# A batched matmul in fp16 on one core: loads six batches ahead, and stores on the loads' queue

## The chip, the core and the metric

The kernel runs on one core of one Trainium2 chip. The core has five engines that run side by side, each with its own stream of instructions: TensorE (PE; its weight loads are shown apart as PEld), VectorE (DVE), ScalarE (ACT), GpSimd (POOL) and SyncE (SP). They meet through semaphores. Tensors lie in HBM; compute reads on-chip memory, and the matmul's results come out in a second, small on-chip memory (PSUM). Data between HBM and the chip are moved by 16 DMA engines, which all five engines can ask for transfers through queues. The metric is the device time of one execution in microseconds (us); lower is better.

## The reference

```
batch, dim_i, dim_j, dim_k = 32, 256, 512, 384
x: (32, 256, 512) float32      y: (32, 512, 384) float32
return np.einsum('bij,bjk->bik', x, y).astype(np.float32)
```

There are 32 independent products of a 256x512 and a 512x384 matrix. Per batch 512 KB of x and 768 KB of y are read and 384 KB of output are written.

## The kernel before

There is one loop over the 32 batches (L43). A batch is handled in five steps.

1. Load. x of the batch goes into `x_sb` (L47), y into `y_sb` (L54), each as one DMA issued by SyncE. A partition, one of 128 rows of on-chip memory, holds two rows of x (4 KB) and four rows of y (6 KB), in either case one unbroken piece of HBM. For the last batch y is loaded as four DMAs, one for each t (L52).
2. Cast. The four slices of y become fp16 in `y_r`, two on ScalarE (L59), two on VectorE (L61).
3. Transpose. TensorE transposes eight 128x128 blocks of x through an identity matrix into PSUM (`t_ps`, L67). VectorE and ScalarE cast the results into `xt_sb` (L73, L75).
4. Multiply. Eight fp16 matmuls add up over t into two PSUM tiles `o_ps` (L84), which ScalarE (L93) and VectorE (L95) copy into `o_sb`.
5. Store. GpSimd issues one DMA of `o_sb` to HBM (L102). For the last batch there are two, one for each half (L100).

Every pool of the loop has eight buffers, apart from the two in PSUM, which have four. The program is written batch by batch, and a scheduler interleaves neighbouring batches on the engines: on VectorE, for instance, the casts of transposed x for one batch stand ahead of the casts of y for it. Each engine then goes through its own list in order and waits where an instruction names a semaphore. SyncE's list holds nothing but loads, GpSimd's (after the identity) nothing but stores.

The DMAs of SyncE use eight semaphores in turn, DMAHW0 to DMAHW7. So a DMA is issued only when the one eight places earlier on that queue has landed, and at most eight are under way. In before that is four batches of loads. GpSimd's stores have their own eight semaphores, DMASW0 to DMASW7.

Of the kernel before, what the change touches and what calls it, by code (L numbers as in the profile page):

```python
# [1 line left out]

# [5 lines left out]


MM_DT = mybir.dt.float16
P = 128


@with_exitstack
def kernel(
    ctx: ExitStack,
    tc: tile.TileContext,
    x: bass.AP,
    y: bass.AP,  # L20
    out: bass.AP,
):
    nc = tc.nc

    B, I, J = x.shape
    _, _, K = y.shape

    NI = I // P
    NJ = J // P

    const_pool = ctx.enter_context(tc.tile_pool(name="const", bufs=1))
    x_pool = ctx.enter_context(tc.tile_pool(name="x_pool", bufs=8))
    y_pool = ctx.enter_context(tc.tile_pool(name="y_pool", bufs=8))
    yr_pool = ctx.enter_context(tc.tile_pool(name="yr_pool", bufs=8))
    xt_pool = ctx.enter_context(tc.tile_pool(name="xt_pool", bufs=8))
    o_pool = ctx.enter_context(tc.tile_pool(name="o_pool", bufs=8))
    tpsum_pool = ctx.enter_context(tc.tile_pool(name="tpsum", bufs=4, space=bass.MemoryType.PSUM))
    opsum_pool = ctx.enter_context(tc.tile_pool(name="opsum", bufs=4, space=bass.MemoryType.PSUM))

    identity = const_pool.tile([P, P], mybir.dt.float32)  # L40
    make_identity(nc, identity)

    for b in range(B):  # L43
        last = b == B - 1

        x_sb = x_pool.tile([P, NI, J], mybir.dt.float32)
        nc.sync.dma_start(out=x_sb, in_=x[b].rearrange("(p r) j -> p r j", p=P))  # L47
        y_sb = y_pool.tile([P, NJ, K], mybir.dt.float32)
        y_src = y[b].rearrange("(q t) k -> q t k", q=P)
        if last:  # L50
            for t in range(NJ):
                nc.sync.dma_start(out=y_sb[:, t], in_=y_src[:, t])  # L52
        else:
            nc.sync.dma_start(out=y_sb, in_=y_src)  # L54

        y_r = yr_pool.tile([P, NJ, K], MM_DT)
        for t in range(NJ):
            if t % 2 == 0:
                nc.scalar.copy(y_r[:, t], y_sb[:, t])  # L59
            else:  # L60
                nc.vector.tensor_copy(y_r[:, t], y_sb[:, t])  # L61

        xt_sb = xt_pool.tile([P, NJ, NI, P], MM_DT)
        for t in range(NJ):
            t_ps = tpsum_pool.tile([P, NI, P], mybir.dt.float32)
            for r in range(NI):
                nc.tensor.transpose(  # L67
                    t_ps[:, r],
                    x_sb[:, r, t::NJ],
                    identity,  # L70
                )
            if t % 2 == 0:
                nc.vector.tensor_copy(xt_sb[:, t], t_ps)  # L73
            else:
                nc.scalar.copy(xt_sb[:, t], t_ps)  # L75

        o_sb = o_pool.tile([P, NI, K], mybir.dt.float32)
        o_ps = [
            opsum_pool.tile([P, K], mybir.dt.float32, name=f"o_ps_{r}", tag="o_ps")
            for r in range(NI)  # L80
        ]
        for t in range(NJ):
            for r in range(NI):
                nc.tensor.matmul(  # L84
                    o_ps[r],
                    xt_sb[:, t, r],
                    y_r[:, t],
                    start=(t == 0),
                    stop=(t == NJ - 1),
                )  # L90
        for r in range(NI):
            if r % 2 == 0:
                nc.scalar.copy(o_sb[:, r, :], o_ps[r])  # L93
            else:
                nc.vector.tensor_copy(o_sb[:, r, :], o_ps[r])  # L95

        out_dst = out[b].rearrange("(p r) k -> p r k", p=P)
        if last:
            for r in range(NI):
                nc.gpsimd.dma_start(out=out_dst[:, r], in_=o_sb[:, r])  # L100
        else:
            nc.gpsimd.dma_start(out=out_dst, in_=o_sb)  # L102


# [1 line left out]
_INS = ['x', 'y']  # L106
_OUTS = [((32, 256, 384), 'float32')]


# [23 lines left out]
```

## Time and profile before

| what | us |
|---|---|
| the runs shown | 140.85, 142.6, 140.8 |
| their median | 140.85 |
| span of the profiled execution, first to last instruction | 139.8 |
| median of the runs less that span | 1.05 |
| PE busy | 90.5 |
| ACT busy | 67.9 |
| DVE busy | 60.5 |

The times listed don't say which run was profiled; the span stands for it. The profile is of one execution. Its page gives the busy time of each engine, a row of 40 slices of the span with the busy share of each in tenths, the DMA queues with their packets, megabytes and share of the 16 DMA engines' time, the chain of work that ended last, the costliest groups of instructions, and the DMA issues with the median time from issue to landing. Other views list the waits (who waited for whom: us in total, times, longest), the instructions in order of time (start, us, engine, line), and the busy time of each engine in chosen stretches. In this last one a row begins with the stretch and its length; then come PE, PEld, DVE, ACT and POOL busy with their counts, the clock that TensorE was granted, the DMA share and GB/s. `SPq` and `POOLq` are the queues of SyncE and GpSimd.

### The profile page before, as it was taken

The page shows a single profiled execution, that of the slowest core. Times are in us where ns is not written, and L with a number is a line of the kernel's source. Part 1 is how long each engine was busy: PE and PEld are TensorE (multiplying, and loading weights), DVE is VectorE, ACT ScalarE, POOL GpSimd, SP SyncE. Part 2 cuts the span into 40 slices and gives each one's busy share as a digit, 9 for nine tenths or more (in the row PEclk, how much of TensorE's full clock was granted, in tenths as well). Part 3 has the DMA queues.
Part 4 walks back from the last instruction along what each step waited for, and adds up shares of the span by engine and source line. Part 5 has one row for each costly group of instructions (what it writes and reads, how often), then busy time and mean ns, then how long its engine had stood idle before and what let it go on. Part 6 is the DMA issues. An engine that isn't in the chain of part 4 may idle for free.

```text
span 139.8 us, 1774 instructions
## 1 busy us (share of the span) xinstructions
PE 90.5 (65%) x512; PEld 64.6 (46%) x512; DVE 60.5 (43%) x160; ACT 67.9 (49%) x161; POOL 18.6 (13%) x39
## 2 busy tenths in 40 slices
PE   0699755477763776774777676776558777764820
PEld 0467543355541554552655444554446355553500
DVE  0346542455541555442555542455534255555420
ACT  3347633446632465453556544465634355565610
POOL 1002210111110111101111110111110111111130
PEclk9999999959999599998699997799997579999996
DMA  4999999999999999999999999999999999999631
GB/s 185 412 426 356 362 410 424 424 417 424 423 412 424 416 416 419 427 416 420 413 423 417 424 416 421 423 414 420 425 419 412 419 421 420 420 422 403 270 155 70
DMA packets 12266, 54.65 MB, mean 391 GB/s; under 512 B 1600, under 2 KB 2112, under 8 KB 12256
## 3 DMA queue, kind: packets, MB, share of 16 engines
q1 hardware_dynamic: 9648, 41.95, 73.9%
q0 software_dynamic: 2608, 12.59, 21.9%
q8 instruction: 4, 0.07, 0.2%
q14 instruction: 6, 0.05, 0.1%
HBM read 41.94 MB, written 12.58 MB: 390 GB/s over the span
## 4 chain that ended last, share of the span: by engine, by line
DMA 87%; issue 5%; PE 3%; SPq 1%; POOL 1%; ACT 0%; POOLq 0%
DMA y_sb<-in_y_dram 87%; PE o_ps L84 1%; PE t_ps L67 1%; SPq L47 1%; SPq L54 0%; POOL out_dram L100 0%; POOL out_dram L102 0%; POOLq L128 0%; ACT y_r L59 0%; ACT xt_sb L75 0%; POOLq L100 0%
## 5 line engine op out<-in xcount | busy, mean ns | idle before, releaser
L84 PE MATMUL o_ps<-y_r,xt_sb 128*128 128x384 f16 x256 | 52.2, 349 | 38.2 <-ACT y_r L59 37.1
L84 PEld LDWEIGHTS <-xt_sb 128*128 128x128 f16 x256 | 25.8, 102 | 57.4 <-issue 40.2
L67 PE MATMUL t_ps<-identity,x_sb 128*128 128x128 f32 x256 | 42.7, 318 | 5.4 <-DMA x_sb<-in_x_dram 5.2
L67 PEld LDWEIGHTS t_ps<-identity,x_sb 128*128 128x128 f32 x256 | 39.2, 213 | 11.7 <-PE o_ps L84 5.9
L95 DVE COPY o_sb<-o_ps 128x384 f32<-128x384 f32 x32 | 17.8, 557 | 48.8 <-issue 36.8
L59 ACT CAST y_r<-y_sb 128x384 f16<-128x384 f32 x64 | 29.8, 511 | 17.0 <-DMA y_sb<-in_y_dram 16.8
L102 POOL DMA_DIRECT2D out_dram<-o_sb x31 | 16.9, 545 | 114.1 <-DVE xt_sb L73 72.8
L93 ACT COPY o_sb<-o_ps 128x384 f32<-128x384 f32 x32 | 15.3, 478 | 33.6 <-issue 26.4
L75 ACT CAST xt_sb<-t_ps 128x256 f16<-128x256 f32 x64 | 23.6, 372 | 15.3 <-PE t_ps L67 12.9
L61 DVE CAST y_r<-y_sb 128x384 f16<-128x384 f32 x64 | 20.5, 361 | 22.3 <-DMA y_sb<-in_y_dram 21.8
L73 DVE CAST xt_sb<-t_ps 128x256 f16<-128x256 f32 x64 | 25.4, 417 | 3.2 <-PE t_ps L67 2.8
L59 ACT ACT_TABLE_LOAD x1 | 1.3, 1283 | 0.7 <-PEq L117 0.7
L100 POOL DMA_DIRECT2D out_dram<-o_sb x2 | 1.1, 539 | 2.5 <-ACT o_sb L93 2.5
masks.py:199 POOL TENSOR_SCALAR_AFFINE_SELECT identity<-identity 128x128 f32<-128x128 f32 x1 | 0.3, 287 | 0.1
masks.py:197 POOL MEMSET identity<- 128x128 f32 x1 | 0.2, 204 | 0.3 <-POOLq L117 0.3
L117 POOL MEMSET const-float32-0.0<- 128x1 f32 x1 | 0.1, 98 | 0.2 <-issue 0.2
L117 POOL MEMSET const-bfloat16-1.0<- 128x1 bf16 x1 | 0.1, 101 | 0.0
L117 POOL MEMSET const-uint8-127<- 128x1 uint8 x1 | 0.1, 101 | 0.0
L117 POOL MEMSET const-float32-1.0<- 128x1 f32 x1 | 0.1, 98 | 0.0
## 6 DMA issues: line engine op xcount, KB each, us to landing
y_sb<-in_y_dram SPq DMA_DIRECT2D x31, 768.0 KB, 16.1
x_sb<-in_x_dram SPq DMA_DIRECT2D x32, 512.0 KB, 16.1
out_dram<-o_sb POOLq DMA_DIRECT2D x31, 384.0 KB, 6.4
y_sb<-in_y_dram SPq DMA_DIRECT2D x4, 192.0 KB, 13.1
out_dram<-o_sb POOLq DMA_DIRECT2D x2, 192.0 KB, 2.2
```

The lines of the kernel that those rows point to most:

```text
L47: nc.sync.dma_start(out=x_sb, in_=x[b].rearrange("(p r) j -> p r j", p=P))
L59: nc.scalar.copy(y_r[:, t], y_sb[:, t])
L61: nc.vector.tensor_copy(y_r[:, t], y_sb[:, t])
L67: nc.tensor.transpose(t_ps[:, r], x_sb[:, r, t::NJ], identity,)
L73: nc.vector.tensor_copy(xt_sb[:, t], t_ps)
L75: nc.scalar.copy(xt_sb[:, t], t_ps)
L84: nc.tensor.matmul(o_ps[r], xt_sb[:, t, r], y_r[:, t], start=(t == 0), stop=(t == NJ - 1),)
L93: nc.scalar.copy(o_sb[:, r, :], o_ps[r])
L95: nc.vector.tensor_copy(o_sb[:, r, :], o_ps[r])
L100: nc.gpsimd.dma_start(out=out_dst[:, r], in_=o_sb[:, r])
L102: nc.gpsimd.dma_start(out=out_dst, in_=o_sb)
L117: nc = _bacc.Bacc("TRN2", target_bir_lowering=False, num_devices=1)
```

## The change

Loads, compute and store of a batch become three functions. Before the loop, loads 0 and 1, the identity matrix, and loads 2 to 5 are issued. Then, for each batch b, the loads of batch b+6 are issued, batch b is computed, and its store is issued, now by SyncE. x and y have nine buffers instead of eight, `y_r` and `xt_sb` four instead of eight. The last batch is no longer cut: its y is one load, its output one store. The arithmetic is untouched.

```diff
-    x_pool = ctx.enter_context(tc.tile_pool(name="x_pool", bufs=8))
-    y_pool = ctx.enter_context(tc.tile_pool(name="y_pool", bufs=8))
-    yr_pool = ctx.enter_context(tc.tile_pool(name="yr_pool", bufs=8))
-    xt_pool = ctx.enter_context(tc.tile_pool(name="xt_pool", bufs=8))
+    x_pool = ctx.enter_context(tc.tile_pool(name="x_pool", bufs=AHEAD + 3))
+    y_pool = ctx.enter_context(tc.tile_pool(name="y_pool", bufs=AHEAD + 3))
+    yr_pool = ctx.enter_context(tc.tile_pool(name="yr_pool", bufs=4))
+    xt_pool = ctx.enter_context(tc.tile_pool(name="xt_pool", bufs=4))
...
-    make_identity(nc, identity)
-    for b in range(B):
-        last = b == B - 1
...
-        nc.sync.dma_start(out=x_sb, in_=x[b].rearrange("(p r) j -> p r j", p=P))
...
-        if last:
-            for t in range(NJ):
-                nc.sync.dma_start(out=y_sb[:, t], in_=y_src[:, t])
-        else:
-            nc.sync.dma_start(out=y_sb, in_=y_src)
+    def load(b):
+        x_sb = x_pool.tile([P, NI, J], F32, name="x_sb")
+        y_sb = y_pool.tile([P, NJ, K], F32, name="y_sb")
+        x_src = x[b].rearrange("(p r) j -> p r j", p=P)
+        y_src = y[b].rearrange("(q t) k -> q t k", q=P)
+        nc.sync.dma_start(out=x_sb, in_=x_src)
+        nc.sync.dma_start(out=y_sb, in_=y_src)
+        loaded[b] = x_sb, y_sb
+    def compute(b):
+        x_sb, y_sb = loaded.pop(b)
...
+        return o_sb
-        if last:
-            for r in range(NI):
-                nc.gpsimd.dma_start(out=out_dst[:, r], in_=o_sb[:, r])
-        else:
-            nc.gpsimd.dma_start(out=out_dst, in_=o_sb)
+    def store(b, o_sb):
+        nc.sync.dma_start(
+            out=out[b].rearrange("(p r) k -> p r k", p=P), in_=o_sb
+        )
+    HEAD = 2
+    load(0)
+    load(1)
+    make_identity(nc, identity)
+    for b in range(HEAD, AHEAD):
+        load(b)
+    for b in range(B):
+        if b + AHEAD < B:
+            load(b + AHEAD)
+        store(b, compute(b))
```

The order of the other engines' instructions is the same as before but for the last batch, where two of VectorE's and two of ScalarE's casts swap places. SyncE's list is where things move. In mid-run it reads as follows before (a row is a line of the kernel, the tile written and the one read, partitions by elements; in brackets what it waits for, where `DMAHW` are the semaphores in turn and the others those of engines that must have let go of a buffer or filled one; the numbers behind names tell buffers and uses apart):

```order
L47 DMA x_sb_564<-in_x_dram 128x1024 [waits DMAHW0_49,PE_49]
L54 DMA y_sb_566<-in_y_dram 128x1536 [waits DMAHW1_49,DVE_49,Activation_49]
L47 DMA x_sb_604<-in_x_dram 128x1024 [waits DMAHW2_49,PE_49]
L54 DMA y_sb_606<-in_y_dram 128x1536 [waits DMAHW3_49,DVE_49,Activation_49]
L47 DMA x_sb_644<-in_x_dram 128x1024 [waits DMAHW4_49,PE_49]
L54 DMA y_sb_646<-in_y_dram 128x1536 [waits DMAHW5_49,DVE_49,Activation_49]
```

These are loads alone, two for each batch, each behind the landing of the load four batches earlier. On SyncE in mid-run of the changed kernel stands:

```order
L97 DMA out_0_dram<-o_sb_454 128x768 [waits DMAHW6_49,DVE_49,Activation_49]
L52 DMA x_sb_468<-in_x_dram 128x1024 [waits DMAHW7_49,PE_49]
L53 DMA y_sb_469<-in_y_dram 128x1536 [waits DMAHW0_49]
L97 DMA out_0_dram<-o_sb_494 128x768 [waits DMAHW1_49,DVE_49,Activation_49]
L52 DMA x_sb_508<-in_x_dram 128x1024 [waits DMAHW2_49,PE_49]
L53 DMA y_sb_509<-in_y_dram 128x1536 [waits DMAHW3_49]
```

Three DMAs now make a batch, and the eight semaphores cover two and two thirds of them. The order is x of b+6, y of b+6, store b, x of b+7. Eight places ahead of store b stands x of b+4, so store b waits for that x to have landed and for both halves of output b to be copied; x of b+6 waits for y of b+3, and y of b+6 for store b-3. The loads behind a store wait with it.

The second place is the end of the program. On SyncE before, the last loads are:

```order
L47 DMA x_sb_1324<-in_x_dram 128x1024 [waits DMAHW6_49,PE_49]
L52 DMA y_sb_1326<-in_y_dram 128x384 [waits DMAHW7_49,DVE_49,Activation_49]
L52 DMA y_sb_1326<-in_y_dram 128x384 [waits DMAHW0_49]
L52 DMA y_sb_1326<-in_y_dram 128x384 [waits DMAHW1_49]
L52 DMA y_sb_1326<-in_y_dram 128x384 [waits DMAHW2_49]
```

After these nothing is left on SyncE's list; the stores are on GpSimd's. On SyncE in the changed kernel the list ends with:

```order
L52 DMA x_sb_1108<-in_x_dram 128x1024 [waits DMAHW7_49,PE_49]
L53 DMA y_sb_1109<-in_y_dram 128x1536 [waits DMAHW0_49]
L97 DMA out_0_dram<-o_sb_1134 128x768 [waits DMAHW1_49,DVE_49,Activation_49]
L97 DMA out_0_dram<-o_sb_1170 128x768 [waits DMAHW2_49,DVE_49,Activation_49]
L97 DMA out_0_dram<-o_sb_1206 128x768 [waits DMAHW3_49,DVE_49,Activation_49]
L97 DMA out_0_dram<-o_sb_1242 128x768 [waits DMAHW4_49,DVE_49,Activation_49]
L97 DMA out_0_dram<-o_sb_1278 128x768 [waits DMAHW5_49,DVE_49,Activation_49]
L97 DMA out_0_dram<-o_sb_1314 128x768 [waits DMAHW6_49,DVE_49,Activation_49]
L97 DMA out_0_dram<-o_sb_1350 128x768 [waits DMAHW7_49,DVE_49,Activation_49]
```

The last x and y are of batch 31; behind them stand seven stores, of batches 25 to 31.

More of the change, by code (lines that the diff above doesn't have):

```diff
@@ L11 @@
 MM_DT = mybir.dt.float16
+F32 = mybir.dt.float32
 P = 128
+AHEAD = 6
 @with_exitstack
@@ L38 @@
     opsum_pool = ctx.enter_context(tc.tile_pool(name="opsum", bufs=4, space=bass.MemoryType.PSUM))
-    identity = const_pool.tile([P, P], mybir.dt.float32)
-    make_identity(nc, identity)
-    for b in range(B):
-        last = b == B - 1
-        x_sb = x_pool.tile([P, NI, J], mybir.dt.float32)
-        nc.sync.dma_start(out=x_sb, in_=x[b].rearrange("(p r) j -> p r j", p=P))
-        y_sb = y_pool.tile([P, NJ, K], mybir.dt.float32)
-        y_src = y[b].rearrange("(q t) k -> q t k", q=P)
-        if last:
-            for t in range(NJ):
-                nc.sync.dma_start(out=y_sb[:, t], in_=y_src[:, t])
-        else:
-            nc.sync.dma_start(out=y_sb, in_=y_src)
-        y_r = yr_pool.tile([P, NJ, K], MM_DT)
+    identity = const_pool.tile([P, P], F32)
+    loaded = {}
+    def load(b):
+        x_sb = x_pool.tile([P, NI, J], F32, name="x_sb")
+        y_sb = y_pool.tile([P, NJ, K], F32, name="y_sb")
+        x_src = x[b].rearrange("(p r) j -> p r j", p=P)
+        y_src = y[b].rearrange("(q t) k -> q t k", q=P)
+        nc.sync.dma_start(out=x_sb, in_=x_src)
[3 more added lines that the diff above has]
+        x_sb, y_sb = loaded.pop(b)
+        y_r = yr_pool.tile([P, NJ, K], MM_DT, name="y_r")
         for t in range(NJ):
@@ L61 @@
                 nc.vector.tensor_copy(y_r[:, t], y_sb[:, t])
-        xt_sb = xt_pool.tile([P, NJ, NI, P], MM_DT)
+        xt_sb = xt_pool.tile([P, NJ, NI, P], MM_DT, name="xt_sb")
         for t in range(NJ):
-            t_ps = tpsum_pool.tile([P, NI, P], mybir.dt.float32)
+            t_ps = tpsum_pool.tile([P, NI, P], F32, name="t_ps")
             for r in range(NI):
[L67 to L71, printed above, removed]
+                nc.tensor.transpose(t_ps[:, r], x_sb[:, r, t::NJ], identity)
             if t % 2 == 0:
@@ L75 @@
                 nc.scalar.copy(xt_sb[:, t], t_ps)
-        o_sb = o_pool.tile([P, NI, K], mybir.dt.float32)
+        o_sb = o_pool.tile([P, NI, K], F32, name="o_sb")
         o_ps = [
-            opsum_pool.tile([P, K], mybir.dt.float32, name=f"o_ps_{r}", tag="o_ps")
+            opsum_pool.tile([P, K], F32, name=f"o_ps_{r}", tag="o_ps")
             for r in range(NI)
@@ L95 @@
                 nc.vector.tensor_copy(o_sb[:, r, :], o_ps[r])
-        out_dst = out[b].rearrange("(p r) k -> p r k", p=P)
-        if last:
-            for r in range(NI):
-                nc.gpsimd.dma_start(out=out_dst[:, r], in_=o_sb[:, r])
-        else:
-            nc.gpsimd.dma_start(out=out_dst, in_=o_sb)
+        return o_sb
[13 more added lines that the diff above has]
+        store(b, compute(b))
 _INS = ['x', 'y']
```

## The prediction

> **What bounds the kernel now.** I read the page first, then the waits of the SyncE queue, then the busy time by stretches, then the last 15 us in order of time. From the page:
>
> ```profile
> span 139.8 us, 1774 instructions
> PE 90.5 (65%) x512; PEld 64.6 (46%) x512; DVE 60.5 (43%) x160; ACT 67.9 (49%) x161; POOL 18.6 (13%) x39
> DMA  4999999999999999999999999999999999999631
> DMA packets 12266, 54.65 MB, mean 391 GB/s; under 512 B 1600, under 2 KB 2112, under 8 KB 12256
> q1 hardware_dynamic: 9648, 41.95, 73.9%
> q0 software_dynamic: 2608, 12.59, 21.9%
> DMA 87%; issue 5%; PE 3%; SPq 1%; POOL 1%; ACT 0%; POOLq 0%
> y_sb<-in_y_dram SPq DMA_DIRECT2D x31, 768.0 KB, 16.1
> x_sb<-in_x_dram SPq DMA_DIRECT2D x32, 512.0 KB, 16.1
> out_dram<-o_sb POOLq DMA_DIRECT2D x31, 384.0 KB, 6.4
> out_dram<-o_sb POOLq DMA_DIRECT2D x2, 192.0 KB, 2.2
> ```
>
> The DMA line is at 9 in 36 of 40 slices, no compute engine is busy for more than 65% of the span, and the chain that ended last is 87% DMA. The loads are q1 (issued by SyncE), the stores q0 (issued by GpSimd). A load lands 16.1 us after its issue, a store after 6.4 us although it was issued later: stores overtake the loads that stand in the other queue.
>
> ```profile
> SPq L54 <- DMA y_sb<-in_y_dram: 44.5, 24, 3.7
> SPq L47 <- DMA x_sb<-in_x_dram: 38.4, 27, 2.0
> SPq L54 <- DVE xt_sb L73: 4.9, 3, 1.7
> ```
>
> The SyncE queue waits almost only for its own earlier loads to land (83 us in these two rows), hardly for a buffer that compute still holds (4.9 us). It issues as fast as transfers end.
>
> ```profile
> 3.50:10.50 7.00, 5.64 (x22) 4.00 (x23) 2.80 (x8) 2.83 (x8) 0.00 (x0) 1.00 1.02 419
> 10.50:17.50 7.00, 5.91 (x40) 4.40 (x39) 4.24 (x11) 4.69 (x12) 1.76 (x3) 1.00 0.99 358
> 60.00:110.00 50.00, 34.16 (x194) 24.52 (x194) 23.06 (x62) 25.91 (x62) 6.48 (x12) 0.90 1.02 419
> 130.00:131.00 1.00, 1.00 (x8) 0.65 (x6) 0.36 (x1) 0.53 (x2) 0.00 (x0) 1.00 1.01 393
> 131.00:132.00 1.00, 1.00 (x9) 0.77 (x9) 1.00 (x4) 1.00 (x3) 0.26 (x1) 1.00 0.55 221
> 132.00:133.20 1.20, 0.75 (x5) 0.30 (x4) 0.13 (x2) 0.60 (x2) 0.28 (x1) 1.00 0.47 186
> 133.20:134.00 0.80, 0.54 (x3) 0.10 (x1) 0.35 (x1) 0.00 (x0) 0.00 (x0) 1.00 0.68 269
> 134.00:135.50 1.50, 0.09 (x1) 0.00 (x0) 0.56 (x1) 0.48 (x1) 0.72 (x2) 1.00 0.00 0
> 135.50:137.30 1.80, 0.00 (x0) 0.00 (x0) 0.00 (x0) 0.00 (x0) 0.35 (x1) 0.95 0.60 219
> ```
>
> The last two columns are the DMA share and GB/s. Loads alone (3.5 to 10.5 us, before any store) move 419 GB/s at a share of 1.02, loads and stores together (60 to 110 us) the same 419: the 16 DMA engines are full with one queue or with two. One stretch (10.5 to 17.5) is slower, 358, while no less busy. From 131 us on the share falls to about half and then to nothing: that is the only idle time, and the only thing a new order of the same bytes can win.
>
> ```profile
> 116.08 5.57 SPq L52 DMA_DIRECT2D y_sb<-in_y_dram  x4
> 124.21 0.63 DVE L61 CAST y_r<-y_sb 128x384 f16<-128x384 f32 x2 [0.35 <-DMA y_sb<-in_y_dram]
> 128.54 0.63 DVE L61 CAST y_r<-y_sb 128x384 f16<-128x384 f32 x2 [1.02 <-DMA y_sb<-in_y_dram]
> 130.64 0.56 DVE L95 COPY o_sb<-o_ps 128x384 f32<-128x384 f32 x1 [1.47 <-issue]
> 133.19 0.36 DVE L61 CAST y_r<-y_sb 128x384 f16<-128x384 f32 x1 [1.07 <-DMA y_sb<-in_y_dram]
> 134.18 0.56 DVE L95 COPY o_sb<-o_ps 128x384 f32<-128x384 f32 x1 [0.63 <-PE o_ps L84]
> 127.41 0.54 POOL L102 DMA_DIRECT2D out_dram<-o_sb  x1 [3.12 <-DVE xt_sb L73]
> 131.74 0.54 POOL L102 DMA_DIRECT2D out_dram<-o_sb  x1 [3.79 <-ACT xt_sb L75]
> 134.78 1.07 POOL L100 DMA_DIRECT2D out_dram<-o_sb  x2 [2.50 <-ACT o_sb L93]
> ```
>
> The last piece of y, issued by 121.65 (116.08 + 5.57), is in use only at 133.19. So between 131 and 133.2 some of the 16 DMA engines have run dry while others still hold load pieces: they do not finish together. Then output 31 is computed (to 134.74) and stored: second half issued at 135.3, landed 2.2 us later, at 137.5. The program ends at 139.8, 2.3 us after that.
>
> **The change, part by part.**
>
> *Stores on the loads' queue, behind load b+6.* In before, stores 0 to 29 have been moved by about 133.2 (store 29: issue 127.41 plus some 6 us), ahead of the last load piece. In the changed order only stores 0 to 24 stand before the last load (the SyncE rows shown with the change); 25 to 31 follow it. The work does not shrink, but seven stores are left to keep the DMA engines full while output 31 is computed. A store costs 21.9% of 139.8 us over 32, that is 0.96 us of every DMA engine. The last engine to finish loads, at 133.19, then has only stores 30 and 31 to do, in one piece: 133.2 + 2 × 0.96 = 135.1 instead of 137.5. Gain 2.4 us. The bounds: no gain at all (below, the rivals), and on the other side 3.8 us, if all engines finish together. For that, from 131 to 137.3 the rows show 221 × 1.0 + 186 × 1.2 + 269 × 0.8 + 0 + 219 × 1.8 = 1,053 KB moved, where 419 GB/s would have moved 2,640: 3.8 us empty. I take 2.4, because the last piece of load shows engines that run behind, and nothing in the change lightens the loads.
>
> *Is store 31 covered?* The last y would land five stores earlier than 133.2, less what dearer stores cost (below): about 128.9. From a whole y to a finished output, before shows 128.54 to 131.20 (130.64 + 0.56), 2.7 us; then 0.3 for the issue and 2.2 for landing, were it alone: 134.1. Behind six other stores it lands at 128.9 + 7 × 0.98 = 135.7. The queue ends last, with 1.6 us to spare, so compute 31, and the y of the last batch no longer being cut into four, cost nothing. That cover is gone if compute takes 4.3 us.
>
> *Packets.* The 1600 packets under 512 B are 16 completions for each of the 100 DMAs. q0 has 2608 packets; without the completions of its 33 DMAs 2080 of data are left, about 6 KB each. q1 has 67 DMAs (31, 32 and the four of the last y), so 1072 completions, and 8576 data packets, which is 128 (one per partition) for each of its 67 DMAs. If stores on q1 also go by one packet per partition row (3 KB), they need 4096: some 2000 more in all. Price: q1 takes 73.9% × 139.8 × 16 / 41.95 = 39.4 us per MB with 230 packets, q0 38.9 with 207. The 0.5 us over 23 packets is 22 ns each, or 2000 × 22 / 16 = 2.7 us per engine: the upper bound. The lower is 0 (bytes alone count). But the slow stretch lies wholly in q1: 7 × (1 − 358/419) = 1.0 us on each engine, 16 of q1's 1653. Without it q1 is at 39.0 per MB, 4 to 5 ns a packet, +0.6 us. I take 0.6. Cutting the last y no more saves 384 packets, 0.1 us at the same price.
>
> *Waits on the SyncE queue.* Store b waits for output b, and loads b+7 stand behind it. It also waits, by the rotation of eight semaphores, until x of b+4 has landed. Batch period: 54.5 MB / 32 / 419 GB/s = 4.07 us; x of b+4 lands some three periods after y of b, 12 us or more. Output b is there 3.2 us after its y (124.21 to 127.41, 128.54 to 131.74). So the wait for compute is over long before the other one, with about 9 us in hand, and costs 0; bounds 0 and, if that slack is gone, the fourth rival. At the start:
>
> ```profile
> 10.80 0.68 POOL L102 DMA_DIRECT2D out_dram<-o_sb  x1 [9.49 <-ACT xt_sb L75]
> 13.57 0.33 SPq L47 DMA_DIRECT2D x_sb<-in_x_dram  x1
> ```
>
> Output 0 is ready at 10.8; the eighth x, which waits for the fourth, is issued at 13.57, and store 0 would wait for that same landing. Even there compute is first.
>
> *Issues, pools, identity.* 32 issues of 0.33 us join SyncE, which spends 83 us waiting: nothing. GpSimd loses 33 issues of 0.54 us, idle time. Nine buffers for x and y instead of eight remove at most the 4.9 us of buffer waits, hidden behind full DMA engines. Four for y_r and xt_sb instead of eight: output b is finished some 3 us after its y, less than one period, so reuse after four periods waits for nothing. The identity is made at the start in both.
>
> Sum against the profiled execution: 139.8 − 2.4 + 0.6 − 0.1 = 137.9. The median of the runs, 140.85, lies 1.05 above that span (140.85 − 139.8); with it, 139.0.
>
> **Rivals.**
>
> *The engines end together* (or the slow stretch does not return). For it: the stretch at 358 GB/s begins as GpSimd issues its first store at 10.8, and this queue goes away. Against: the stretch has loads alone in its first half, and later stores slow nothing (419). Gain 3.8 instead of 2.4: 137.6; with the stretch gone too (1.0): 136.6. The Trainium skill bears on this: "DMA: Bandwidth & Descriptors", Latency and other measured facts, says that two of the 16 DMA engines are usually slower and guesses at the descriptor rings of GpSimd's DMAs as the cause. By that rule, all stores on SyncE would even out the engines, which is this rival's 137.6; no row here tells which engine is behind.
>
> *Stores in bursts are dearer* (the other side). Now stores trickle in among loads; afterwards all engines write at once. In the one stretch with stores alone (135.5 to 137.3) a share of 0.60 moved 219 GB/s, 365 per full share, against 419/1.02 = 411: 12.6% dearer. On all stores: 32 × 0.96 × 0.126 = 3.9 us, 142.9. It decides from 1.85 us on, 6% per store. Against it: those last pieces have rows half as long (192 KB in 128 rows).
>
> *Nothing changes.* The Trainium skill, same page, Issuing engines are not separate DMA queues, states that DMAs run on the same 16 engines and interleave whoever issues them, so that spreading them saves issue time alone; by it, moving them back together should leave 140.85. The rows agree in mid-run (419 either way). As a mechanism of this kernel: the end stays empty because the store of batch 31 is late after all, compute taking over 4.3 us from the last y.
>
> *SyncE is held up* by a late output, and loads behind it start late. It decides when output b needs over 12 us after its y; each further us would cost about 1 us per batch, up to 32 us. Nothing here is near that.
>
> **How the numbers follow.** The forecast, 139.0, has 0.42 (its own range 138.1 to 140.4); engines ending together 0.32; dearer bursts 0.16; no change 0.07; SyncE held up 0.03. The range 136.7 to 142.4 leaves out the last, the upper part of the bursts and a tip of the first rival. Two per cent, about what a measurement of this kernel can tell from no change, puts the borders at 138.0 and 143.7. Faster: 0.30 of the first rival and 0.05 of the forecast, 0.35. Slower: 0.05 of bursts with a higher packet price and 0.03, 0.08. Within: 0.57.
>
> **What the changed profile would show.** Right: no q0; the DMA line at 9 until about four us before the end; the last y landing near 129; waits of SyncE for DMAs, not for DVE or ACT copies into o_sb; stores landing in 10 us or more, not 6. Packets of about 3 KB confirm the +2000. Wrong: under 415 GB/s in mid-run (bursts, or packets), a share that falls well before the last store (not covered), or no ragged end at all (engines even).

## The result, and the profile after

The changed kernel takes 137.22 us (median of 4 runs, 137.07 to 137.32) against 140.82 before (median of 4, 140.69 to 142.6): a ratio of 0.970, with a 95% interval of 0.965 to 0.976. It is faster by 3.0%. The forecast of 139.0 was 1.8 us too slow; 137.2 lies in the stated range, but the prediction gave only 0.35 to a gain of over 2%.

The page of the changed kernel, in the same rows as before:

```profile
span 135.3 us, 1733 instructions
PE 85.9 (63%) x512; PEld 59.4 (44%) x512; DVE 63.3 (47%) x160; ACT 68.9 (51%) x161; POOL 0.7 (1%) x6
DMA  4999999999999999999999999999999999999993
DMA packets 13833, 54.64 MB, mean 404 GB/s; under 512 B 1536, under 2 KB 1536, under 8 KB 13824
q1 hardware_dynamic: 13824, 54.53, 98.8%
y_sb<-in_y_dram SPq DMA_DIRECT2D x32, 768.0 KB, 11.2
x_sb<-in_x_dram SPq DMA_DIRECT2D x32, 512.0 KB, 10.2
out_dram<-o_sb SPq DMA_DIRECT2D x32, 384.0 KB, 10.9
```

All transfers of the three tensors are on q1. The DMA line stays at 9 for 38 slices instead of 36, and a store now lands 10.9 us after its issue instead of 6.4: it waits its turn. There are 13824 packets on q1, 96 DMAs with 16 completions and 128 data packets each, so a store does go by one packet per partition row.

Busy time by stretches (columns as before: PE, PEld, DVE, ACT, POOL, clock, DMA share, GB/s):

```profile
10.50:17.50 7.00, 5.83 (x40) 4.23 (x39) 4.32 (x12) 4.72 (x13) 0.00 (x0) 1.00 1.03 422
17.50:30.00 12.50, 9.26 (x63) 7.17 (x62) 6.75 (x19) 7.58 (x19) 0.00 (x0) 1.00 1.01 405
60.00:110.00 50.00, 33.07 (x199) 22.24 (x198) 24.61 (x61) 26.14 (x62) 0.00 (x0) 1.00 1.02 419
129.00:131.00 2.00, 1.08 (x7) 0.43 (x5) 0.56 (x1) 0.48 (x1) 0.00 (x0) 1.00 1.04 416
131.00:132.00 1.00, 0.00 (x0) 0.00 (x0) 0.00 (x0) 0.00 (x0) 0.00 (x0) 1.00 0.86 341
132.00:133.00 1.00, 0.00 (x0) 0.00 (x0) 0.00 (x0) 0.00 (x0) 0.00 (x0) 1.00 0.78 310
133.00:134.00 1.00, 0.00 (x0) 0.00 (x0) 0.00 (x0) 0.00 (x0) 0.00 (x0) 0.61 0.37 147
```

Mid-run is the same 419 GB/s. Stores alone (129 to 131) move 416. The falling share at the end is now the only ragged part; the empty 1.5 us of before (134.0 to 135.5) is gone. The stretch at 358 GB/s has left its place (422 there now), but 17.5 to 30 is at 405.

The end in order of time (start, us, engine, line), VectorE and then SyncE's queue:

```profile
128.07 0.63 DVE L63 CAST y_r<-y_sb 128x384 f16<-128x384 f32 x2 [0.41 <-DMA y_sb<-in_y_dram]
130.11 0.56 DVE L93 COPY o_sb<-o_ps 128x384 f32<-128x384 f32 x1 [1.41 <-PE o_ps L82]
118.06 13.00 SPq L97 DMA_DIRECT2D out_dram<-o_sb  x7
```

The last y is in use at 128.07 instead of 133.19. Seven stores are issued between 118.06 and 131.06; the last of them waits for output 31 (130.67) and is there 3.7 us after its issue, at 134.5. The program ends 0.8 us later, at 135.3. Before, 2.2 us lay between the last landing (137.59) and the end (139.76).

SyncE's waits in the changed kernel (us in total, times, longest):

```profile
SPq L52 <- DMA y_sb<-in_y_dram: 36.1, 24, 1.9
SPq L97 <- DMA x_sb<-in_x_dram: 22.8, 26, 0.9
SPq L97 <- DVE o_sb L93: 6.0, 2, 3.7
SPq L97 <- ACT o_sb L91: 5.9, 23, 0.3
SPq L136 <- PEq L136: 0.6, 2, 0.4
```

It waits for transfers; for outputs only twice, at stores 30 and 31, which have no load behind them. The row that names ScalarE's copies is no wait for outputs, since these had long been copied: output 10, for one, was complete at 45.5 and its store went out at 57.2. The last row is SyncE at the exit (L136), waiting for the other engines. The same row before, from the same view of that kernel, reads:

```profile
SPq L128 <- PEq L128: 1.8, 2, 1.3
```

### The profile page after: what moved, and what is told of

The parts are those of the page before. It is cut to its first block, busy times and chain, and to the rows that moved or that the text cites. A ratio compares the mean times of both kernels' runs of the same rounds, so it can differ in the third digit from the quotient of the medians.

```text
span 135.3 us, 1733 instructions
## 1 busy us (share of the span) xinstructions
PE 85.9 (63%) x512; PEld 59.4 (44%) x512; DVE 63.3 (47%) x160; ACT 68.9 (51%) x161; POOL 0.7 (1%) x6
## 2 busy tenths in 40 slices
DMA packets 13833, 54.64 MB, mean 404 GB/s; under 512 B 1536, under 2 KB 1536, under 8 KB 13824
## 3 DMA queue, kind: packets, MB, share of 16 engines
q1 hardware_dynamic: 13824, 54.53, 98.8%
## 4 chain that ended last, share of the span: by engine, by line
DMA 73%; PE 12%; DVE 5%; ACT 4%; SPq 2%; issue 1%; ACTq 0%
DMA y_sb<-in_y_dram 40%; DMA out_dram<-o_sb 33%; PE o_ps L82 10%; DVE xt_sb L71 3%; ACT y_r L61 3%; DVE y_r L63 2%; PE t_ps L69 1%; ACT o_sb L91 1%; SPq L52 1%; DVE o_sb L93 1%; SPq L53 1%; ACT xt_sb L73 0%; ACTq L61 0%
## 5 line engine op out<-in xcount | busy, mean ns | idle before, releaser
L82 PE MATMUL o_ps<-y_r,xt_sb 128*128 128x384 f16 x256 | 48.2, 331 | 35.2 <-ACT y_r L61 30.6
L82 PEld LDWEIGHTS <-xt_sb 128*128 128x128 f16 x256 | 25.0, 98 | 51.9 <-issue 35.7
L69 PE MATMUL t_ps<-identity,x_sb 128*128 128x128 f32 x256 | 39.2, 297 | 8.9 <-DMA x_sb<-in_x_dram 8.8
L69 PEld LDWEIGHTS t_ps<-identity,x_sb 128*128 128x128 f32 x256 | 34.7, 210 | 18.3 <-PE o_ps L82 13.4
L71 DVE CAST xt_sb<-t_ps 128x256 f16<-128x256 f32 x64 | 26.6, 423 | 4.6 <-PE t_ps L69 4.1
## 6 DMA issues: line engine op xcount, KB each, us to landing
out_dram<-o_sb SPq DMA_DIRECT2D x32, 384.0 KB, 10.9
```

Source lines behind the costliest of these rows:

```text
L69: nc.tensor.transpose(t_ps[:, r], x_sb[:, r, t::NJ], identity)
L82: nc.tensor.matmul(o_ps[r], xt_sb[:, t, r], y_r[:, t], start=(t == 0), stop=(t == NJ - 1),)
```

## The experiments

Times are compared by their ratio to the kernel before, run on the same chip in the same batch (medians there: 141.35 for e1 to e4, 141.56 for the rest).

### Which part of the change wins: the queue, the last store, or the order

**e1**, all stores back on GpSimd, the rest as changed:

```diff
     def store(b, o_sb):
-        nc.sync.dma_start(
+        nc.gpsimd.dma_start(
```

> The changed kernel with every store issued by GpSimd again; loads, pools and the uncut last batch stay as changed. Theory A (the order on one queue wins: stores that wait behind loads keep the DMA engines full at the end): the whole win goes, 140.3 to 141.2 us, as before the change. Theory B (the win is GpSimd's absence: no drain after its DMAs at the exit, no slow stretch at the first store; order matters little): also back near 140.8, but then the trace shows the slow stretch near 360 GB/s between 10 and 18 us and a GpSimd drain that ends after SyncE is done. Theory C (uncut last batch, nine buffers or the earlier loads win by themselves): it stays near 137.2.

Measured: 142.63 us, ratio 1.011 (1.005 to 1.016). SyncE's exit wait in e1, one of its stretches, and VectorE's use of the last y:

```profile
SPq L136 <- PEq L136: 1.4, 2, 0.9
```

```profile
10.50:17.50 7.00, 5.41 (x36) 3.87 (x36) 4.43 (x13) 4.63 (x13) 1.76 (x3) 1.00 1.00 357
```

```profile
132.34 0.63 DVE L63 CAST y_r<-y_sb 128x384 f16<-128x384 f32 x2 [0.25 <-ACT xt_sb L73]
```

Earlier loads, more buffers and an uncut last batch win nothing by themselves; theory C falls. It is 1.1% slower than before. What it has of the change that can cost is the last batch in one piece, since y is usable only when all of it is there and nothing hides the compute then; no run separates that. The last y comes late, as theory A has it, and the exit wait and the stretch at 357 GB/s are back, as B has it: this run does not tell the two apart.

**e2** and **e3**, one store only on GpSimd, the last or the fourth:

```diff
-        nc.sync.dma_start(
+        eng = nc.gpsimd if b == B - 1 else nc.sync    # e3: b == 3
+        eng.dma_start(
```

> The changed kernel with store 31 alone issued by GpSimd; stores 0 to 30 stay on SyncE behind the loads. Theory A: the order of the rest is kept, so at most 0.5 us is lost: 137.2 to 137.7. Theory B: GpSimd's drain is back on the path at the end; in the kernel before, 1.4 us of its last 2.3 us (last landing at 137.5, end at 139.8, against 134.5 and 135.3 after) would be that drain: 138.3 to 138.8.

> The changed kernel with store 3 alone issued by GpSimd, about 115 us before the end. If GpSimd's drain costs only shortly after a DMA of its own: 137.2 (137.0 to 137.4). If having issued any DMA makes its exit slow: 138.0 to 138.7. If the slow stretch near 360 GB/s belongs to GpSimd's first store, it shows between 15 and 30 us, and 0.5 to 1 us is added.

Measured: e2 137.44 us, ratio 0.975 (0.971 to 0.979); e3 137.73, 0.976 (0.972 to 0.980). Neither costs a whole microsecond. In e2 GpSimd issues its store at 131.41, while earlier ones are still being moved, so that its way out overlaps the transfers and SyncE's exit wait (next row) stays short: theory B's 138.3 was wrong in that place. e3 loses 0.5 us, as much as I had expected of the slow stretch at the least: where the changed kernel moves 405 GB/s, e3 moves 390 (second row), which is 12.5 × 15 / 419 = 0.4 us. Its end comes 0.9 us after its last landing, so a DMA that GpSimd issues early does not slow the exit. SyncE's exit wait in e2, and that stretch in e3:

```profile
SPq L137 <- PEq L137: 0.6, 2, 0.5
```

```profile
17.50:30.00 12.50, 9.24 (x62) 6.98 (x61) 6.47 (x18) 7.04 (x17) 0.69 (x1) 1.00 1.01 390
```

**e5**, and again **e12** beside the changed kernel: the kernel before with nothing changed but the issuer of its last two half stores.

```diff
             for r in range(NI):
-                nc.gpsimd.dma_start(out=out_dst[:, r], in_=o_sb[:, r])
+                nc.sync.dma_start(out=out_dst[:, r], in_=o_sb[:, r])
```

> The kernel before with only the two half stores of batch 31 moved from GpSimd to SyncE, whose list is empty by then. Theory D (a GpSimd DMA keeps GpSimd in its exit drain for 3 to 4 us after its issue, so the kernel before ends 1.3 us later than its last landing requires): the stores land when they did, and the end follows 0.8 to 0.9 us after the last landing instead of 2.2: 1.2 to 1.5 us less than before, 139.3 to 139.7 against 140.8. Theory A alone (only the order matters): no change, within 0.4 us of before.

> e5 again beside e9 and the kernel before. Theory D: 1.2 to 1.9 us less than before; what then still separates it from e9, 1.8 to 2.6 us, is the order of the stores (with the smaller slow stretch).

Measured: 139.78, ratio 0.984 (0.979 to 0.989), and 139.58, 0.987 (0.981 to 0.992): 1.8 and 2.0 us less than before. In e5, SyncE's exit wait and the landing of these stores:

```profile
SPq L128 <- PEq L128: 0.7, 2, 0.5
```

```profile
DMA to landing us min/median/max: 1.9/1.9/1.9
```

The longest exit wait falls from 1.3 to 0.5 us, and the stores land in 1.9 us instead of 2.2, from issues 0.3 us earlier (134.53 and 134.98 in its trace, 134.78 and 135.31 before). That is more than the exit alone, which was all that I had expected. No store was moved past a load here. So about half of what the change won has nothing to do with the order of the other stores.

**e6**, all stores on GpSimd but late, and **e11**, the same with stores 30 and 31 on SyncE. Store b is held until x of batch b+5 has landed (`xs` keeps the x tiles):

```diff
     def store(b, o_sb):
+        if b < B - 1:
+            gate = gate_pool.tile([P, 1], F32, name="gate")
+            nc.gpsimd.tensor_scalar_mul(gate, xs[min(b + 5, B - 1)][:, 0, 0:1], 0.0)
+            nc.gpsimd.tensor_add(o_sb[:, 0, 0:1], o_sb[:, 0, 0:1], gate)
-        nc.sync.dma_start(
+        nc.gpsimd.dma_start(        # e11: nc.sync for b >= B - 2
```

> All stores on GpSimd as in e1, but store b (b below 31) is held until x of batch b+5 (at most 31) has landed: GpSimd takes one column of that x times 0 and adds it to one column of the output. So stores come late although their queue is GpSimd's; two stores (30 and 31) go out last. Theory A (late stores win, whatever queue): the last y lands near 128 to 129.5 us instead of 132.2 in e1, and the total falls from 142.6 to 138.3 to 139.5, the rest to 137.2 being GpSimd's drain and the second store at the end. Theory B' (GpSimd's queue itself is slow): it stays over 141. The slow stretch moves with the first store, to where that is.

> e6 (GpSimd's stores held back until a later x has landed) with stores 30 and 31 issued by SyncE. Theory D (GpSimd's exit drain): SyncE's longest wait at the exit for another engine falls from 0.9 to about 0.4, and the total from 139.9 to between 138.2 and 138.9. If e6 lost its time to held-back stores alone: 139.6 or more.

Measured: e6 139.94, ratio 0.988 (0.985 to 0.991); e11 138.46, 0.979 (0.974 to 0.984). VectorE's use of the last y, SyncE's exit wait and one stretch in e6, then the exit wait in e11:

```profile
129.07 0.63 DVE L65 CAST y_r<-y_sb 128x384 f16<-128x384 f32 x2 [0.77 <-DMA y_sb<-in_y_dram]
```

```profile
SPq L142 <- PEq L142: 1.4, 2, 0.9
```

```profile
126.00:130.00 4.00, 2.33 (x18) 1.83 (x16) 1.85 (x5) 2.15 (x5) 3.17 (x12) 1.00 0.71 279
```

```profile
SPq L143 <- PEq L143: 0.7, 2, 0.5
```

Against e1, late stores on the very same queue win 2.3 points of ratio (1.011 to 0.988, about 3 us), and the last y is usable at 129.07 instead of 132.34: the order wins, whichever queue holds it. About 0.7 us of this is the smaller slow stretch (409 GB/s from 17.5 to 30 in e6, 357 from 10.5 to 17.5 in e1). e6 was 0.4 us slower than I had expected: with the gate on the last x, the last stores go out so late that the DMA share falls to 0.71 between 126 and 130. Moving the last two to SyncE wins 1.5 us more, with the exit wait down as in e5.

### How many stores must stand behind the last load

**e10**, **e7**, **e8** and **e4** change only the distance (the buffers stay nine, eleven in e10), with **e9**, the changed kernel itself, beside e10:

```diff
-AHEAD = 6
+AHEAD = 8      # e10;  4: e7,  3: e8,  2: e4
```

> The changed kernel once more, so that it stands beside e10, e11 and e12 on one chip. 137.0 to 137.8, a ratio of 0.970 to 0.976 to before.

> The changed kernel with loads eight batches ahead (eleven buffers), nine stores behind the last load. Theory A: with seven stores the last output is already covered, so two more win nothing: within 0.3 us of e9. If a later store as such wins: 0.6 to 1 us less.

> Loads four batches ahead (five stores behind the last load). Theory A with the changed kernel's own rows: last y 2 x 0.93 us later than 128.0, at 129.8; output 31 2.7 us later, its store landed 2.2 to 2.5 us after that, near 134.9 instead of 134.5: 137.2 to 137.9 us. If earlier loads as such win: clearly more, over 138.5.

> Loads three batches ahead (four stores behind the last load). Theory A: last y at 130.8, output 31 at 133.5, landed near 135.8 to 136: 138.2 to 138.9 us, if mid-run stays at 419 GB/s. If SyncE is already held up by outputs at this depth as in e4 (where it waited for outputs 84 us in all), mid-run falls and it is nearer to 140.

> The changed kernel with loads two batches ahead instead of six (nine buffers kept). Three stores instead of seven stand behind the last load. Theory A: in mid-run nothing changes (419 GB/s, SyncE held up at most briefly), but the last y lands four stores later, 128.0 + 4 x 0.93 = 131.7; output 31 is there 2.7 us later and its store lands 2.2 us after its issue, 136.7 instead of 134.5: 139.2 to 139.8 us. Theory B (GpSimd's absence wins): 137.2 to 137.6. If a store that waits for its output holds up the loads behind it already at this depth: well over 140, with idle DMA in mid-run.

| run | stores behind the last load | us | ratio | 95% interval |
|---|---|---|---|---|
| e10 | 9 | 137.39 | 0.971 | 0.966 to 0.977 |
| e9 | 7 | 137.25 | 0.970 | 0.966 to 0.975 |
| e7 | 5 | 137.85 | 0.973 | 0.971 to 0.976 |
| e8 | 4 | 138.79 | 0.981 | 0.977 to 0.984 |
| e4 | 3 | 142.5 (140.82, 140.86, 144.14, 146.5) | | |

VectorE's first use of the last y, in e10, e7, e8 and e4 in turn:

```profile
126.40 0.63 DVE L63 CAST y_r<-y_sb 128x384 f16<-128x384 f32 x2 [0.43 <-DMA y_sb<-in_y_dram]
```

```profile
130.22 0.63 DVE L63 CAST y_r<-y_sb 128x384 f16<-128x384 f32 x2 [0.41 <-DMA y_sb<-in_y_dram]
```

```profile
131.82 0.63 DVE L63 CAST y_r<-y_sb 128x384 f16<-128x384 f32 x2 [0.43 <-DMA y_sb<-in_y_dram]
```

```profile
133.29 0.63 DVE L63 CAST y_r<-y_sb 128x384 f16<-128x384 f32 x2 [0.42 <-DMA y_sb<-in_y_dram]
```

With 128.07 for seven stores, every store taken from behind the last load puts that load 0.8 to 1.6 us later. With five stores or fewer the end follows the compute of batch 31; from seven up the number no longer matters (e9 and e10 are equal within 0.3 us). That is the cover which the prediction worked out: output 31 needs some 2.7 us and an issue and landing of more than 2, and seven stores of 0.94 us (384 KB at 419 GB/s) hide it. e7 and e8 lie within their expectations. e4 does not: its fastest execution is 1 us over the 139.8, and its times no longer agree. SyncE's wait for outputs in e4 (the changed kernel has 6.0, 2, 3.7 in this row):

```profile
SPq L97 <- DVE o_sb L93: 83.8, 32, 6.5
```

All 32 stores wait for their output, and the loads wait behind them; so they do in e8, for 58.3 us in all. The waits that the prediction ruled out for six ahead are real at three and at two. But from 60 to 110 us both kernels move 420 GB/s all the same, so that the waits cost nothing there. What e4 loses lies earlier:

```profile
17.50:30.00 12.50, 8.80 (x41) 5.52 (x39) 3.98 (x10) 4.58 (x12) 0.00 (x0) 0.75 0.98 384
30.00:60.00 30.00, 19.60 (x121) 13.82 (x120) 15.47 (x39) 15.96 (x39) 0.00 (x0) 0.99 1.02 411
60.00:110.00 50.00, 32.38 (x195) 22.06 (x195) 24.91 (x62) 26.52 (x62) 0.00 (x0) 1.00 1.02 420
```

Against 419 GB/s that is 1.0 us in the first row and 0.6 in the second, where the changed kernel loses 0.4 in its slow stretch: about the 1 us by which e4 misses. What of it is the hold-up, and what the slow stretch, no run separates.

### The slow stretch

The stretch near 358 GB/s was suspected to be GpSimd's. It is not: e8 has no GpSimd store at all, and shows

```profile
10.50:17.50 7.00, 5.92 (x39) 4.41 (x38) 4.33 (x12) 4.71 (x13) 0.00 (x0) 1.00 1.02 373
```

In e8 the first store is issued earlier than with six ahead, and the stretch is earlier too; with six ahead it lies in 17.5 to 30. In every kernel here but e4 it begins one to four us before the first packet of a store. Its cost against 419 GB/s is 7 × (1 − 358/419) = 1.0 us before, 12.5 × (1 − 405/419) = 0.4 us after. What causes it stays open.

## Why the prediction was wrong

**The step that failed** is the one that was left out of the sum: "The program ends at 139.8, 2.3 us after that". I carried these 2.3 us over as if they belonged to any kernel, and put GpSimd's part at "GpSimd loses 33 issues of 0.54 us, idle time". They were mostly GpSimd's. The end of the chain of work before had said so (start, us, what):

```profile
134.78 0.54 POOL out_dram L100
135.32 0.53 POOLq L128
```

The chain does not end in a transfer, but in GpSimd's exit (L128). The trace has there, right behind its last store, an instruction of GpSimd named DRAIN, which takes 3.7 us, from 135.27 to 138.99. GpSimd's drains at the exit line (times, shortest, median and longest in ns, first and last start) in before, e5 and the changed kernel in turn:

```profile
L128 POOLq DRAIN  x3: 40/102/3715, 135.3 to 139.5; - x3
```

```profile
L128 POOLq DRAIN  x3: 40/102/3922, 131.7 to 137.7; - x3
```

```profile
L136 POOLq DRAIN  x3: 34/78/389, 1.0 to 135.0; - x3
```

In before, the last store lands at 137.59, SyncE has confirmed all transfers at 137.8, and the exit barrier waits until 139.0. In e5 the long drain is as long, but it starts at 131.7 and is over before the last landing at 136.9; the changed kernel has none at its end. In e1 it takes 4.0 us, in e2 3.3, in e6 4.1. Where SyncE issues the last store, the end comes 0.8 to 1.3 us after the last landing (the changed kernel, e4, e5, e11, e12) instead of 2.1 to 2.2 (before, e1, e6). In e2, where GpSimd issues it but the transfers go on nearly as long as the drain, it comes 1.0 us after: the drain is only paid for where no transfer covers it.

**The sum, term by term**, on the profiled executions (139.8 to 135.3, 4.5 less where 1.9 was forecast). *Order, −2.4:* right in kind, and shown by e6 against e1 and by the row of distances. On one chip, e9 lies 2.3 us under e12, which has the order of before and the exit of after; that is the order together with the packets and the slow stretch. *Packets, +0.6:* not seen as a loss. q1 takes 98.8% × 135.3 × 16 / 54.53 = 39.2 us per MB, both queues of before 39.3, while the slow stretch became 0.6 us cheaper, so the two about cancel. *Exit, 0:* should have been −1.3 (from 2.17 to 0.83 in the two traces); this is half of the missing 2.6 us, and its largest part. The other half is the last landing itself, at 134.5 where the sum has 135.7 (137.6 − 1.9): 0.6 us of it is the smaller slow stretch; the last 0.6 no run separates.

**A second term was mis-sized too.** I took 1.05 us for what lies around the span. Where the runs list both, a time lies 1.8 above its span (137.07 and 135.3; a run of before with 141.56 and 139.8). If that holds for the profiled execution of before, it stood for about 141.6, 0.8 above the median, and the forecast put on it is 0.8 too low. This hid part of the error: without it the forecast would have been 139.7.

**What held.** Mid-run is full with one queue as with two, 419 GB/s. Store 31 is covered: the last store is issued as soon as output 31 is there, and 416 GB/s flow meanwhile. SyncE is not held up (6 us in two waits, both behind the last load). The last batch in one piece costs nothing under that cover.

**The rivals.** *Engines end together* gave 137.6, near the measured time, but not by its mechanism: the share still falls over three microseconds at the end. Its sentence from the Trainium skill ("DMA: Bandwidth & Descriptors", Latency and other measured facts), on two slower DMA engines and GpSimd's descriptor rings, is neither borne out nor refuted, as no row tells which engine is late. *Dearer bursts* falls: stores alone move 416 GB/s at a share of 1.04, that is 400 per full share against 411, or 3% dearer and not 12.6%. *Nothing changes* falls. The Trainium skill ("DMA: Bandwidth & Descriptors", Issuing engines are not separate DMA queues) says that issuing DMAs from several engines at once saves issue time alone; the 419 either way agrees, for bandwidth. But e5 changes the issuer of two DMAs and nothing else, and wins 1.8 us, of which the earlier issue is a small part. *SyncE held up*: its waits are there at three and two batches ahead, but mid-run moves 420 GB/s with them, and nothing of the size that the prediction named was seen.

No version tried beats the changed kernel; e10 equals it.

## What to carry to other kernels

When the DMA engines are full all along, what an order of the same transfers can win is at the ends: keep enough stores behind the last load to hide the compute of the last tile (here seven of 0.94 us against some 5 us), and no more is needed. Look up what the last microseconds before the end consist of, and who is still at work when the last transfer has landed, before they go into a sum as a constant. And where one queue carries both loads and stores, look whether a store's output is there when its turn comes: here, at three batches or fewer, SyncE waits for outputs at every store, yet only at two was the time longer than the late last load explains.

## What the runs showed that I had not expected

- A DMA that GpSimd issues near the end of the program keeps it in its exit drain for 3.3 to 4.1 us after the issue, here up to 1.4 us beyond the landing of that same DMA.
- Around the first store the transfers have a slow stretch, on either queue, at 0.3 to 1.0 us in all.
- The runs of before spread from 140.5 to 142.8, many of them near 140.7 or 141.6; the changed kernel's do not (137.06 to 137.32 in both sets). Nothing here explains it.
